# One decoder trunk on one core: maxima's rows handed on one step later, outputs' low halves subtracted by VectorE

## Chip, core and metric

The kernel runs on one core of one Trainium2 chip. The metric is the device time of one execution in microseconds (us), and the time of a kernel is the median of its runs. Engines are named as the profile names them: PE (TensorE matmuls), PEld (its weight loads), DVE (VectorE), ACT (ScalarE), POOL (GpSimd), SP (SyncE, which only issues DMAs here). A profile is one execution, recorded.

## What is computed

A two-layer trunk over 2048 tokens of width 1024: a Mamba-2 mixer, then an attention mixer with 16 heads, 64 + 32 channels for queries and keys and 64 for values, and a final RMS norm. The change touches the causal attention alone, which the reference writes in blocks of 128 queries:

```python
    for i in range(S // Q_BLOCK):
        q0 = i * Q_BLOCK
        kv_len = q0 + Q_BLOCK
        s = jnp.einsum('bqhd,bkhd->bhqk', q_nope[:, q0:kv_len], k_nope[:, :kv_len]) + \
            jnp.einsum('bqhr,bkr->bhqk', q_rope[:, q0:kv_len], k_rope[:, :kv_len])
        s = s.astype(jnp.float32) * scale
        mask = (q0 + local)[:, None] >= jnp.arange(kv_len)[None, :]
        p = jax.nn.softmax(jnp.where(mask, s, -jnp.inf), axis=-1).astype(v.dtype)
        outs.append(jnp.einsum('bhqk,bkhd->bqhd', p, v[:, :kv_len]))
```

The output of a head is later multiplied by a gate and by the output weights. Float32 accuracy is kept by halves: a float32 value is stored as a high float16 part and a low one, its rest, and a product is three matmuls (high by high, high by low, low by high).

## The kernel before

The attention stage is the function `heads`. A job is a head h and a block qb of 512 queries, so a head has four jobs; a step of the main loop handles two key blocks of 128 of one job, so the jobs have 2, 4, 6 and 8 steps and a head has 20. There are 320 steps. The engines' instructions stand in the order in which this function issues them. One step does, mixed with each other:

- **scores** of this step's two key blocks: PE computes transposed scores into bank `s` (lines 1388 to 1390, the causal mask by line 1392), ACT takes the exponential into `x` (1394) and casts it to the high half of `PTs` (1399). The low half is `x` minus the high half, `lows` (1412): POOL does it, 512 columns an instruction; for the steps on the diagonal DVE does it, one step later (896 columns, then 384).
- **values**, two steps behind the scores: PE multiplies `PTs` with the head's values into `o` (1427 to 1429).
- **maxima** of later jobs, eight steps ahead of their scores: PE computes plain scores of 128 queries by up to 512 keys into one of the six `s` banks (1266), DVE reduces them to running minima of the negated scores in `mx` (1268). A bank is free again when DVE is through.
- at the end of the step, `waiting()`, what earlier steps put off to this one.

What is put off, before the change. When the last maximum of job n is made in step k: in step k+1 `part_peaks` splits the four numbers into halves in a small tile `nm` (ACT 1275, then POOL 1276); in step k+2 `rows` turns this tile on DVE (1280, `rT<-nm`) and SP writes it to DRAM (1281, `m_d<-rT`); in step k+3 SP reads it back as two rows of the query tile (1289, `xT<-m_d`), from where the score matmuls add it.

When the last values of a job are done in step k, `finish` computes the reciprocal of the sum and the output `On` on DVE (1443, 1447). In step k+2 ACT casts it to the high half of `Op` (1451) and POOL subtracts to get the low half (1452). For the second head of a pair, in step k+4, `turn` has SP transpose `Op` by a DMA into `Os` (1461). Two steps later POOL adds the two halves to `Of` (1464), and three steps after the turning SP stores it (1470, `o_d<-Of`); the stores of head 13 also load a piece of the output weights (1240, `wr<-in_mla_w_out`), which the last stage, `back`, splits into `W` and `K` halves on ACT (1546) and DVE (1547) while the last heads still run. When the last values of head h are done, SP loads the keys and values of head h+2 into the same buffer (1217, 1218, 1223).

Every engine and SP's queue work in order, so a wait holds up what stands behind it.

Of the kernel before, what the change touches and what calls it, by code (L numbers as in the profile page):

```python
# [13 lines left out]
F16 = mybir.dt.float16  # L14
I32 = mybir.dt.int32
AF = mybir.ActivationFunctionType
ALU = mybir.AluOpType
# [4 lines left out]
P = 128  # L22
# [47 lines left out]
class Net:  # L70
# [1253 lines left out]
    def heads(self, sp):  # L1324
        nc, v, act, mm = self.nc, self.nc.vector, self.nc.scalar.activation, self.nc.tensor.matmul
# [12 lines left out]
        for n, (h, qb) in enumerate(jobs):  # L1338
            for j in range(4):
                parts = self.cuts(qb, j)  # L1340
# [7 lines left out]
        for i in range(len(duos) - 2, -1, -1):  # L1348
            n, kb = duos[i + 1]
# [5 lines left out]
        def bank():  # L1355
            return self.t(self.ap, "s", [P, TB], bufs=6)

        def maxima(n, j, i, c0, w, last):

            h, qb = jobs[n]  # L1360
            if (j, i) == (0, 0):
                peak[n] = self.t(sp, "mx", [P, 4, 4], bufs=4)
                if n + 2 < len(jobs):
                    self.load_q(*jobs[n + 2])
            Q, K, qs = quer[h, qb], keys[h % 2], slice(j * P, (j + 1) * P)
            junk = self.t(sp, "junk", [P, TB], BF16, bufs=1)
            self.peaks(bank(), Q[:, 0, qs], K[:, 0, c0:c0 + w], fence, junk, peak[n], i, j, last)
            if last and j == 3:
                u, e, Q = turned[n % 3], peak.pop(n)[:, i], quer[h, qb]
                given[n] = [(step[0] + 1, lambda: self.part_peaks(e, u)),  # L1370
                            (step[0] + 2, lambda: self.rows(n, u, self.t(sp, "rT", [P, 32], F16, bufs=2), None)),
                            (step[0] + 3, lambda: self.set_rows(n, Q))]

        def scores(n, kb):

# [38 lines left out]
        def values(n, kb, u):  # L1414

            h, qb = jobs[n]
            V = vals[h % 2]
            if kb == 0:
                outs[n] = self.t(self.ap, "o", [P, 4, P], bufs=2)
            for b in range(2):  # L1420
                k = kb + b
                jj = max(k - 4 * qb, 0)
                for j in range(jj, 4):
                    o = outs[n][:, j]
                    at = TB + (j - jj) * P if b else j * P
                    hi, lo = u[:, 0, at:at + P], u[:, 1, at:at + P]
                    mm(o[:, 0:64], hi, V[:, k, 0:64], start=k == 0 and j == 0, stop=False, skip_group_check=True)  # L1427
                    mm(o[:, 0:65], hi, V[:, k, 64:129], start=False, stop=False, skip_group_check=True)  # L1428
                    mm(o[:, 0:65], lo, V[:, k, 64:129], start=False, stop=k == 4 * qb + j, skip_group_check=True)  # L1429
                if b == 0:  # L1430
                    yield
            if kb == 4 * qb + 2:
                finish(n)
            if kb == 4 * NB - 2 and h + 2 < NH:
                self.load_k(h + 2, 0, NB)
                self.load_v(h + 2)

        def finish(n):

            h, qb = jobs[n]  # L1440
            O = outs.pop(n)
            ri = self.t(sp, "ri", [P, 4], bufs=2)
            v.reciprocal(ri, O[:, :, 64])
            if (h // 2, qb) not in pairs:
                pairs[h // 2, qb] = self.t(sp, "Op", [P, 2, 4, P], F16, bufs=6)
            o = self.t(sp, "On", [P, 4, 64], bufs=3)
            v.tensor_tensor(o, O[:, :, 0:64], ri.unsqueeze(2).to_broadcast([P, 4, 64]), ALU.mult)
            hi, lo = (pairs[h // 2, qb][:, m, :, h % 2 * 64:(h % 2 + 1) * 64] for m in range(2))

            def parts():  # L1450
                act(hi, o, AF.Copy)
                nc.gpsimd.tensor_tensor(lo, o, hi, ALU.subtract)

            later.append((step[0] + 2, parts))
            if h % 2:
                later.append((step[0] + TURN + 1, lambda: turn(h, qb)))

        def turn(h, qb):

            o = self.t(sp, "Os", [P, 2, TB], F16, bufs=2)  # L1460
            nc.sync.dma_start_transpose(o.rearrange("p m (j t) -> p (m j) t", j=4),
                                        pairs.pop((h // 2, qb)).rearrange("p m j c -> p (m j c)"))
            whole = self.t(sp, "Of", [P, TB], bufs=2)
            later.append((step[0] + 2, lambda: nc.gpsimd.tensor_tensor(whole, o[:, 0], o[:, 1], ALU.add)))
            later.append((step[0] + 3, lambda: store(h, qb, whole)))

        def store(h, qb, o):

            r0 = (h // 2) * P
            nc.sync.dma_start(self.o_d[r0:r0 + P, qb * TB:(qb + 1) * TB], o)  # L1470
            if h == NH - 3:
                self.load_wo(qb)

        step, later, held, fresh, made, given = [0], [], [], [], ends[2], {}
# [18 lines left out]
        def some(due):  # L1493

            nonlocal made
            while cols[made] < due:
                maxima(*chunks[made])
                made += 1
# [229 lines left out]
```

## Time and profile before

| | |
|---|---|
| median of 3 runs | 2894.04 us (2892.67 to 2894.78) |
| profiled execution | 2886.88 us, of which the span from first to last instruction is 2885.1 us |
| mean granted TensorE clock | 0.994 of full speed |
| busy in the span | PE 97%, PEld 56%, DVE 74%, ACT 63%, POOL 33% |
| the attention stage | from about 1975 us to about 2695 us of the span |

Times in rows of the trace are microseconds from the start of the span. Matmuls overlap: one of 512 columns is recorded with 0.38 us though the next may start 0.22 us after it, so a wait of PE shows as idle time only from the end of the last matmul.

### The profile page before, as it was taken

The page shows a single profiled execution, that of the slowest core. Times are in us where ns is not written, and L with a number is a line of the kernel's source. Part 1 is how long each engine was busy: PE and PEld are TensorE (multiplying, and loading weights), DVE is VectorE, ACT ScalarE, POOL GpSimd, SP SyncE. Part 2 cuts the span into 40 slices and gives each one's busy share as a digit, 9 for nine tenths or more (in the row PEclk, how much of TensorE's full clock was granted, in tenths as well). Part 3 has the DMA queues.
Part 4 walks back from the last instruction along what each step waited for, and adds up shares of the span by engine and source line. Part 5 has one row for each costly group of instructions (what it writes and reads, how often), then busy time and mean ns, then how long its engine had stood idle before and what let it go on. Part 6 is the DMA issues. An engine that isn't in the chain of part 4 may idle for free. (4 is left out here: it accounts for less than half of the span.)

```text
span 2885.1 us, 58276 instructions
## 1 busy us (share of the span) xinstructions
PE 2793.3 (97%) x21170; PEld 1623.6 (56%) x21170; DVE 2124.8 (74%) x5114; ACT 1830.9 (63%) x3989; POOL 961.3 (33%) x1080
## 2 busy tenths in 40 slices
PE   7899999999999999999999999999999999998998
PEld 3465556554555554454555545545666666665787
DVE  7789987787777878879775455357788878878454
ACT  8777655576566766556554344335889888898422
POOL 0221221211121211223221121224778777786300
PEclk9999999999999999999999999999999999999999
DMA  8765736455464567636646988872333324333553
GB/s 292 252 201 197 219 118 208 142 179 183 162 226 132 176 192 223 214 116 209 219 138 231 264 264 247 258 225 68 81 67 73 78 65 88 78 77 99 171 210 110
DMA packets 361156, 487.01 MB, mean 169 GB/s; under 512 B 179490, under 2 KB 224322, under 8 KB 359428
## 3 DMA queue, kind: packets, MB, share of 16 engines
q1 hardware_dynamic: 349732, 447.37, 51.7%
q0 software_dynamic: 11136, 35.92, 3.4%
q8 instruction: 166, 2.72, 0.4%
q14 instruction: 122, 1.00, 0.1%
HBM read 332.83 MB, written 123.34 MB: 158 GB/s over the span
## 5 line engine op out<-in xcount | busy, mean ns | idle before, releaser
L1412 POOL TENSOR_TENSOR PTs<-x,PTs 128x512 f16<-128x512 f32 (+1 forms) x380 | 444.4, 1194 | 135.8 <-ACT PTs L1399 91.3
L1394 ACT ACTIVATE x<-s 128x512 f32<-128x512 f32 (+3 forms) x640 | 326.5, 523 | 70.5 <-PE s L1390 42.8
L86 PE MATMUL mm<-xT,wsp 128*128 128x512 f16 x800 | 305.5, 382 | 5.5 <-ACT wsp L117 5.2
L87 PE MATMUL mm<-xT,wsp 128*128 128x512 f16 x800 | 304.8, 381 | 0.0
L88 PE MATMUL mm<-xT,wsp 128*128 128x512 f16 x800 | 304.0, 380 | 0.0
L1399 ACT ACTIVATE PTs<-x 128x1024 f16<-128x1024 f32 (+1 forms) x320 | 297.2, 929 | 9.9
L1268 DVE CUSTOM_DVE_ANT_0 junk<-s,fence,mx 128x512 bf16<-128x512 f32 (+1 forms) x372 | 241.0, 648 | 47.8 <-PE s L1266 16.9
L1429 PE MATMUL o<-K,PTs 128*128 128x65 f16 x2176 | 263.3, 193 | 4.1 <-DVE PTs L1412 1.7
L1427 PE MATMUL o<-K,PTs 128*128 128x64 f16 x2176 | 265.9, 192 | 0.0
L1428 PE MATMUL o<-K,PTs 128*128 128x65 f16 x2176 | 265.6, 194 | 0.0
L839 POOL TENSOR_TENSOR Xp<-Xw,Xp 128x512 fp32r<-128x512 f32 x64 | 90.6, 1416 | 505.9 <-ACT Xp L838 279.9
L86 PE MATMUL mm<-wsp,xT 128*128 128x512 f16 (+1 forms) x640 | 230.6, 362 | 3.5 <-ACT craw L643 3.4
L87 PE MATMUL mm<-wsp,xT 128*128 128x512 f16 (+1 forms) x640 | 231.2, 361 | 2.1 <-DVE wsp L118 2.1
L1428 PEld LDWEIGHTS <-PTs 128*128 128x128 f16 x2176 | 203.1, 97 | 53.0 <-issue 0.5
L1427 PEld LDWEIGHTS <-PTs 128*128 128x128 f16 x2176 | 205.0, 97 | 49.4 <-issue 2.0
L649 DVE SCALAR_TENSOR_TENSOR cacc<-craw,pack,cacc 128x512 f32<-128x512 f32 x288 | 215.8, 779 | 22.9 <-ACT cacc L647 21.6
L88 PE MATMUL mm<-wsp,xT 128*128 128x512 f16 (+1 forms) x640 | 231.1, 361 | 0.0
L1388 PE MATMUL s<-xT,K 98*128 98x512 f16 (+1 forms) x628 | 219.3, 349 | 10.8 <-DVE mx L1268 6.2
L1389 PE MATMUL s<-xT,K 96*128 96x512 f16 (+1 forms) x628 | 219.5, 350 | 0.0
L1266 PE MATMUL s<-K,xT 96*128 96x512 f16 (+1 forms) x616 | 213.6, 349 | 5.2 <-ACT nm L1275 2.0
L1390 PE MATMUL s<-xT,K 96*128 96x512 f16 (+1 forms) x628 | 217.9, 347 | 0.0
L1429 PEld LDWEIGHTS <-PTs 128*128 128x128 f16 x2176 | 201.7, 98 | 6.7 <-DVE PTs L1412 3.8
(480 smaller groups left out, 7272.1 us busy)
## 6 DMA issues: line engine op xcount, KB each, us to landing
wsp<-wi_d SPq DMA_DIRECT2D x96, 512.0 KB
big<-cumT SPq DMA_DIRECT2D x64, 512.0 KB
wraw<-in_ssm_w_out_dram SPq DMA_DIRECT2D x96, 256.0 KB
wi_d<-wsp SPq DMA_DIRECT2D x32, 512.0 KB
wsp<-wo_d SPq DMA_DIRECT2D x32, 512.0 KB
wsp<-wu_d SPq DMA_DIRECT2D x28, 512.0 KB
hx<-in_ssm_w_in_dram SPq DMA_DIRECT2D x48, 256.0 KB
wraw<-in_ssm_w_in_dram SPq DMA_DIRECT2D x48, 256.0 KB
```

The costliest lines, as they stand in the source:

```text
L86: mm(out, l_hi, r_hi, start=start, stop=False)
L87: mm(out, l_hi, r_lo, start=False, stop=False)
L88: mm(out, l_lo, r_hi, start=False, stop=stop)
L1268: self.nc.vector.tensor_tensor_reduce(junk[:, :w], s[:, :w], fence[:, at:at + w], -1.0 / MSCALE, peak[:, i - 1, j:j + 1] if i else 3.0e38, ...
L1388: mm(s, K[0:98, 0, ks], Q[0:98, 0, c], start=True, stop=False)
L1389: mm(s, K[0:96, 0, ks], Q[0:96, 1, c], start=False, stop=False)
L1394: act(o, s, AF.Exp)
L1399: act(u[:, 0, at:end], x[:, at:end], AF.Copy)
L1412: engine.tensor_tensor(u[:, 1, a:b], x[:, a:b], u[:, 0, a:b], ALU.subtract)
L1427: mm(o[:, 0:64], hi, V[:, k, 0:64], start=k == 0 and j == 0, stop=False, skip_group_check=True)
L1428: mm(o[:, 0:65], hi, V[:, k, 64:129], start=False, stop=False, skip_group_check=True)
L1429: mm(o[:, 0:65], lo, V[:, k, 64:129], start=False, stop=k == 4 * qb + j, skip_group_check=True)
```

## The change

The transposition of the maxima moves from two to three steps behind and the reading of the rows from three to four. The low half of the outputs is made by DVE, one step after ACT's high half. The two turned halves are added three steps after the turning, and stored four after. There is one more buffer for `On`.

```diff
-                            (step[0] + 2, lambda: self.rows(n, u, self.t(sp, "rT", [P, 32], F16, bufs=2), None)),
-                            (step[0] + 3, lambda: self.set_rows(n, Q))]
+                            (step[0] + 3, lambda: self.rows(n, u, self.t(sp, "rT", [P, 32], F16, bufs=2), None)),
+                            (step[0] + 4, lambda: self.set_rows(n, Q))]
...
-            o = self.t(sp, "On", [P, 4, 64], bufs=3)
+            o = self.t(sp, "On", [P, 4, 64], bufs=4)
...
-            def parts():
-                act(hi, o, AF.Copy)
-                nc.gpsimd.tensor_tensor(lo, o, hi, ALU.subtract)
-
-            later.append((step[0] + 2, parts))
+            later.append((step[0] + 2, lambda: act(hi, o, AF.Copy)))
+            later.append((step[0] + 3, lambda: v.tensor_tensor(lo, o, hi, ALU.subtract)))
...
-            later.append((step[0] + 2, lambda: nc.gpsimd.tensor_tensor(whole, o[:, 0], o[:, 1], ALU.add)))
-            later.append((step[0] + 3, lambda: store(h, qb, whole)))
+            later.append((step[0] + 3, lambda: nc.gpsimd.tensor_tensor(whole, o[:, 0], o[:, 1], ALU.add)))
+            later.append((step[0] + 4, lambda: store(h, qb, whole)))
```

Lines behind line 1450 stand three lower in the changed kernel (1464 becomes 1461), and 1451 and 1452 become 1450 and 1451. PE's order is the same in both programs.

The place where one pair of heads passes to the next comes once in two heads. On DVE, before:

```order
L1268 ISA junk_27417,mx_27345<-s_27418,fence_21736,mx_27345 128x128
...
L1268 ISA junk_27429,mx_27345<-s_27430,fence_21736 128x512
...
L1268 ISA junk_27452,mx_27345<-s_27453,fence_21736,mx_27345 128x512
...
L1280 STREAM_TRANSPOSE rT_27468<-nm_4122_21732 128x32
L1268 ISA junk_27482,mx_27345<-s_27483,fence_21736,mx_27345 128x512
...
L1412 TENSOR_TENSOR PTs_27422<-x_27421,PTs_27422 128x896
L1268 ISA junk_27528,mx_27345<-s_27529,fence_21736,mx_27345 128x256
```

The same place on DVE after the change:

```order
L1451 TENSOR_TENSOR Op_26295<-On_27260,Op_26295 128x4x64
L1268 ISA junk_27417,mx_27344<-s_27418,fence_21736,mx_27344 128x128
...
L1268 ISA junk_27429,mx_27344<-s_27430,fence_21736 128x512
...
L1268 ISA junk_27452,mx_27344<-s_27453,fence_21736,mx_27344 128x512
...
L1268 ISA junk_27479,mx_27344<-s_27480,fence_21736,mx_27344 128x512
...
L1412 TENSOR_TENSOR PTs_27422<-x_27421,PTs_27422 128x896
L1280 STREAM_TRANSPOSE rT_27515<-nm_4122_21732 128x32
```

The transposition moved behind one reduction and one subtraction of 896 columns, and a low half of the outputs came in three reductions ahead of it.

SP's queue at the same passing, before:

```order
L1281 DMA m_d<-rT_27468 128x32
L1461 DMA_TRANSPOSE Os_27471<-Op_26297 128x8x128
L1289 DMA xT_26815<-m_d 1x16x32 x2
L1470 DMA o_d<-Of_27473 128x512
L1217 DMA K_3902_20566<-kn_d 64x4096
L1218 DMA K_3902_20566<-kr_d 32x4096
L1223 DMA K_3902_20566<-v_d 128x16x128
L1233 DMA xT_27786<-qn_d 64x2x512
```

And after, on SP:

```order
L1458 DMA_TRANSPOSE Os_27468<-Op_26295 128x8x128
L1281 DMA m_d<-rT_27515 128x32
L1289 DMA xT_26815<-m_d 1x16x32 x2
L1217 DMA K_3902_20566<-kn_d 64x4096
L1218 DMA K_3902_20566<-kr_d 32x4096
L1223 DMA K_3902_20566<-v_d 128x16x128
L1467 DMA o_d<-Of_27470 128x512
L1233 DMA xT_27786<-qn_d 64x2x512
```

The turning went ahead of the maxima's write, and the store of the sum went from ahead of the key and value loads to behind them.

The third place is on ACT where the last pair of heads begins, and the first piece of the last stage's weights (`W<-wr`) stands among the exponentials. Before:

```order
L1394 ACTIVATE x_35353<-s_35355 128x512
L1394 ACTIVATE x_35353<-s_35370 128x512
L1546 ACTIVATE W_37186<-wr_35351 128x2x512
L1399 ACTIVATE PTs_35354<-x_35353 128x1024
L1394 ACTIVATE x_35397<-s_35399 128x512
```

On ACT after the change, rows that begin with the same exponentials and go on until that piece:

```order
L1394 ACTIVATE x_35350<-s_35352 128x512
L1394 ACTIVATE x_35350<-s_35367 128x512
L1399 ACTIVATE PTs_35351<-x_35350 128x1024
...
L1399 ACTIVATE PTs_35582<-x_35581 128x1024
L1394 ACTIVATE x_35634<-s_35636 128x512
L1543 ACTIVATE W_37186<-wr_35391 128x2x512
L1394 ACTIVATE x_35634<-s_35655 128x512
```

The piece moved from row 2692 of ACT to row 2712, into the step six steps later. On DVE its low half moved likewise, from ahead of the other seven such instructions of this stretch to among them: before, those seven stand within 26 rows of DVE, after it all eight stand within 51.

## The prediction

> **What bounds the kernel now.** I read the busy time by stretch first, then who waits for whom in the steady part, then the timeline where those waits are longest. By stretch (length, busy time of PE, PEld, DVE, ACT, POOL with counts, granted clock, DMA share, GB/s):
>
> ```profile
> 2000.00:2600.00 600.00, 591.88 (x7969) 387.03 (x7968) 477.52 (x1358) 530.68 (x925) 467.54 (x463) 1.00 0.35 74
> 2605.00:2610.00 5.00, 1.97 (x22) 1.11 (x21) 2.30 (x8) 1.68 (x2) 0.00 (x0) 0.87 1.00 245
> 2610.00:2615.00 5.00, 4.14 (x41) 3.16 (x41) 4.08 (x10) 4.91 (x10) 4.54 (x5) 0.50 0.88 139
> 2630.00:2635.00 5.00, 3.83 (x46) 2.23 (x45) 4.79 (x8) 3.43 (x7) 2.23 (x3) 1.00 0.86 297
> 2635.00:2640.00 5.00, 3.24 (x20) 1.62 (x20) 5.00 (x10) 4.30 (x6) 4.50 (x4) 0.94 0.47 133
> 2640.00:2645.00 5.00, 5.00 (x50) 2.72 (x48) 4.97 (x12) 4.70 (x8) 4.08 (x4) 0.72 0.60 195
> 2660.00:2695.00 35.00, 32.41 (x504) 22.26 (x503) 20.99 (x34) 33.44 (x58) 33.02 (x27) 1.00 0.19 40
> ```
>
> PE is the bound: 591.88 of 600 us. So the change can win only the time in which PE stands, and removing waits of DVE or POOL is worth nothing unless PE waits for them. Who waits, 2000 to 2600 (total us, times, longest):
>
> ```profile
> DVE rT L1280 <- POOL nm L1276: 47.6, 28, 2.3
> DVE junk L1268 <- PE s L1266: 28.8, 80, 0.5
> POOL Of L1464 <- PE s L1266: 15.6, 4, 3.9
> POOL Of L1464 <- DMA Os<-Op: 8.2, 2, 4.2
> PEld L1389 <- issue: 5.7, 19, 1.0
> PEld L1266 <- issue: 5.2, 5, 1.6
> PEld L1429 <- DVE PTs L1412: 2.4, 9, 0.5
> PE s L1388 <- DVE mx L1268: 2.7, 9, 0.9
> PE s L1266 <- DMA K<-kr_d: 0.5, 1, 0.5
> ```
>
> PE's idle time is 600 - 591.88 = 8.1 us; its weight loader, whose records do not overlap, stands 5.7 + 5.2 + 2.4 = 13.3 us. The truth lies between, nearer to 13.3, because the tail of a matmul's record covers some of each stall. Of it 8.1 (5.7 + 2.4) is DVE being late: a bank not yet reduced, a low half not yet made. 5.2, in five stalls, is PE waiting for the next head's keys. So why is DVE late? The passing from one pair of heads to the next shows it:
>
> ```profile
> 2240.75 0.09 DVE L1268 DVE_READ_ACCUMULATOR2_ANT mx<- 128x1 f32 x1
> 2242.90 0.19 POOL L1276 TENSOR_TENSOR nm<-mx,nm 128x4 f16<-128x4 f32 x1
> 2243.12 0.21 DVE L1280 STREAM_TRANSPOSE rT<-nm 128x32 f16<-128x32 f16 x1 [2.29 <-POOL nm L1276]
> 2243.36 0.33 SPq L1281 DMA_DIRECT2D m_d<-rT  x1
> 2243.78 1.99 SPq L1461 DMA_TRANSPOSE Os<-Op  x1
> 2243.92 1.09 DVE L1412 TENSOR_TENSOR PTs<-x,PTs 128x896 f16<-128x896 f32 x1
> 2246.17 0.55 DVE L1412 TENSOR_TENSOR PTs<-x,PTs 128x384 f16<-128x384 f32 x1
> 2247.27 1.15 POOL L1464 TENSOR_TENSOR Of<-Os 128x512 f32<-128x512 f16 x1 [4.18 <-DMA Os<-Op]
> 2247.31 2.06 DVE L1412 TENSOR_TENSOR PTs<-x,PTs 128x896 f16<-128x896 f32 x1
> 2248.44 0.34 SPq L1470 DMA_DIRECT2D o_d<-Of  x1
> 2248.88 0.52 SPq L1217 DMA_DIRECT2D K<-kn_d  x1
> 2337.04 0.52 SPq L1217 DMA_DIRECT2D K<-kn_d  x1
> 2344.54 0.22 PE L1266 MATMUL s<-K,xT 96*128 96x128 f16 x1 [0.87 <-ACT nm L1275]
> ```
>
> DVE stands 2.29 us for a POOL result that queues behind POOL's subtractions. SP then turns late, POOL waits 4.18 for the turned tile, its addition meets DVE's subtraction (2.06 instead of 1.09), and the store that follows holds the key loads. Two heads later the keys issued at 2337.04 are wanted 7.5 us on, and PE stands 0.87. (A step is (2337.04 - 2248.88) / 40 = 2.2 us.)
>
> **The change, part by part.** *Transposition one step later.* The longest wait, 2.3 us, is about one step, and POOL also loses the outputs' low half. So I cost the 47.6 us at nothing from here on. DVE then reaches its diagonal subtractions up to 2 us earlier; next late would be ACT's cast that feeds them.
>
> *Low half on DVE.* No row shows it. By the clean rows 896 columns take 1.09 and 384 take 0.55, so 1.05 ns a column: 256 columns take 0.55 - 128 x 1.05 ns = 0.42 us. What it can wait for POOL shows in the groups of the steady part:
>
> ```profile
> L1412 DVE TENSOR_TENSOR PTs<-x,PTs 128x896 f16<-128x896 f32 x54 | 71.5, 1323 | 0.0
> L1412 DVE TENSOR_TENSOR PTs<-x,PTs 128x384 f16<-128x384 f32 x53 | 35.6, 672 | 0.0
> L1452 POOL TENSOR_TENSOR Op<-On,Op 128x256 f16<-128x256 f32 x54 | 46.3, 858 | 2.5 <-ACT Op L1451 2.4
> L1412 POOL TENSOR_TENSOR PTs<-x,PTs 128x512 f16<-128x512 f32 x328 | 377.3, 1175 | 100.9 <-ACT PTs L1399 77.0 <-issue 11.8 <-POOL nm L1276 9.9
> ```
>
> DVE's subtractions average 0.23 and 0.12 us above clean, and the worst above (2.06) lost 0.97. So 54 low halves cost DVE from 54 x 0.42 = 23 to 54 x (0.42 + 0.97) = 75 us; I take 0.3 us of waiting, since POOL is busy 78% (467.54 of 600): 39 us, less than the 47.6 it gets back. POOL loses 46.3. The cover is DVE's idle time; if it were gone, each low half would hold the bank of the reduction behind it.
>
> The Trainium skill, page "SBUF — State Buffer", section "Who interferes with whom", states that a VectorE instruction with two SBUF inputs and a GpSimd instruction that reads SBUF exclude each other, the second one fully blocked until the first ends. The 2.06 row, begun 0.04 us after POOL's addition, agrees. The rule speaks against this part: by it each low half that meets POOL waits out POOL's instruction, and the 75 us end would be the one to take; that is the first rival below.
>
> *Addition and store one step later, turning ahead of `m_d`.* The turned tile has landed when POOL comes to it, so the 4.18 us hole and the collision behind it go. The key loads no longer stand behind the store: in their place counts `m_d`, a reading back of the rows, then the keys, and I expect them some 2 us earlier in the odd heads. In the even heads, where no store stood ahead, `m_d` comes under 1 us later. Of the 8.1 us I take 6, of the 5.2 I take 2.5: **-8.5** in the steady part, bounds 0 and -13.3.
>
> *The last stage's first weights on ACT.* These are the rows of the largest stall:
>
> ```profile
> 2602.35 0.60 ACT L1394 ACTIVATE x<-s 128x512 f32<-128x512 f32 x1 [0.46 <-PE s L1390]
> 2603.15 0.41 SPq L1240 DMA_DIRECT2D wr<-in_mla_w_out_dram  x1
> 2608.32 1.06 ACT L1546 ACTIVATE W<-wr 128x1024 fp32r<-128x1024 f32 x1 [5.38 <-DMA wr<-in_mla_w_out_dram]
> 2610.86 0.48 PE L1388 MATMUL s<-xT,K 98*128 98x384 f16 x1 [3.50 <-ACT x L1394]
> ```
>
> ACT stands 5.38 us for a weight load, PE 3.50 behind it, and then the granted clock is 0.50 for five microseconds. The load needs 5.2 us (2603.15 to 2608.32). After the change it is issued behind the key loads, a step or so later, but ACT asks six steps (13 us) later, so it has landed. PE's loss here is (5 - 1.97) + (5 - 4.14) idle and half of 4.14 to the clock: 6.0. I take **-5.5**, bounds -6.0 and 0.
>
> *The other weights, 2630 to 2645.* PE loses 1.17 + 1.76 idle and 0.28 x 5 = 1.4 to the clock, 4.3 in all, with DVE busy 4.8 to 5.0 of 5. The eight extra instructions on DVE stand twice as wide now, but one more is among them, with the low halves, and weights whose store is a step later may hold ACT again: **-1**, bounds -4.3 and +3.
>
> *The end of attention.* PE idles 35 - 32.41 = 2.6 from 2660 to 2695, partly for POOL's subtractions; POOL loses its low halves, DVE gains them with 14 us free: **-0.5**, bounds -2.6 and +1.5. The last chain:
>
> ```profile
> 2696.54 2.84 DVE L1547 TENSOR_TENSOR K<-wr,K 128x1024 fp32r<-128x1024 f32 x2 [0.45 <-ACT K L1546]
> 2696.89 1.40 POOL L1452 TENSOR_TENSOR Op<-On,Op 128x256 f16<-128x256 f32 x1 [0.62 <-ACT Op L1451]
> 2698.32 1.23 SPq L1461 DMA_TRANSPOSE Os<-Op  x1
> ```
>
> The low half now stands on DVE between the two weight halves: the first ends at about 2697.7, plus 0.42 gives 2698.1 instead of 2698.3: **-0.3**, bounds -0.5 and +1.
>
> The buffer more for `On` costs nothing. Sum: -8.5 - 5.5 - 1 - 0.5 - 0.3 = -15.8. The profiled execution took 2886.88 us (span 2885.1), 7.2 below the median of the runs, so the sum gives 2871.1 for such an execution; the same difference on the median of 2894.04 is **2878.2**.
>
> **Rivals.** *Slower: POOL blocks the low halves.* DVE's waits now are 47.6 + 28.8 = 76.4 us, 1.41 for each of the 54 low halves; from there on DVE has nothing left, and 0.42 + 0.97 = 1.39 is close to it. Two of a head's four stand where DVE reduces bank after bank; if 27 of them hold PE for 1 us each, and the steady gain is nil, the time is 2894 + 27 - 7.3 = 2914. For it: POOL's 78%. Against: the present subtractions lose 0.12 and 0.23 on average, not 0.97.
>
> *The keys take over.* With DVE's waits gone PE wants the keys sooner, and in every head they now follow a later `m_d` and its reading back. If the odd heads keep their 2.5 and the seven even ones stand 0.9 each: -15.8 + 2.5 + 6.3 = -7.0, or 2887. For it: 5.2 us of such stalls now. Against: only five waits in some 14 heads (600 us by 20 steps of 2.2), and the store no longer delays the loads.
>
> *The weight stall only moves.* The load issued later and behind the keys keeps ACT standing, there or at the next piece: -15.8 + 5.5 + 1.5 = -8.8, or 2885. Against: 13 us of later asking beside a load of 5.2.
>
> **How the numbers follow.** Forecast 0.68, keys 0.14, weights 0.10, slower 0.08. The modest ends of the terms (-2, -4, +2, +0.5, 0) give 2890.5, the good ends (-12, -6, -3, -1.5, -0.5) give 2871; both middle rivals lie inside, and only the slow one outside: 2870 to 2890. About 0.2%, 5.8 us, is what a measurement of this kernel can tell from no change, so faster means below 2888.2: nearly all of the forecast and over half of the two middle rivals, 0.81; same 0.12; slower 0.07.
>
> **What would show it.** The wait of `rT` for `nm` falls from 47.6 to under 5 us; the low half on DVE averages below 0.8 us; POOL's wait for `Os` is gone; the weight loader's three waits sum to under 6; ACT's 5.38 us wait and the 0.50 clock near 2610 are gone. I am wrong if the low halves average 1.2 us or more, if PE's stalls ahead of line 1266 grow in even heads, or if a wait for `wr` of several microseconds stands on ACT at another place.

## The result and the profile after

The changed kernel takes 2876.62 us (median of 6 runs, 2872.23 to 2877.95) against 2894.84 us (6 runs, 2892.67 to 2900.98): ratio 0.9931, 95% interval 0.9919 to 0.9944. That is 18.2 us less; forecast were 15.8 less. The profiled execution of the changed kernel took 2876.48 us, its span 2874.7.

The saving is split by three marks that both traces have: the first exponential of the stage, the first one of head 13, and the last one. The two rows of each kernel are the group of all 640 exponentials (shortest, median and longest duration in ns, first and last start) and the timeline at head 13. Before:

```profile
L1394 ACT ACTIVATE x<-s x640: 265/578/602, 1976.7 to 2693.2; 128x512 f32<-128x512 f32 x160
2554.34 0.60 ACT L1394 ACTIVATE x<-s 128x512 f32<-128x512 f32 x1 [0.30 <-PE s L1392]
```

After:

```profile
L1394 ACT ACTIVATE x<-s x640: 267/579/603, 1982.0 to 2680.5; 128x512 f32<-128x512 f32 x160
2547.39 0.60 ACT L1394 ACTIVATE x<-s 128x512 f32<-128x512 f32 x1 [0.30 <-PE s L1392]
```

| stretch (us) | before | after | difference | forecast |
|---|---|---|---|---|
| heads 0 to 12 (first exponential to head 13) | 577.6 | 565.4 | -12.2 | -8.5 |
| heads 13 to 15 (to the last exponential) | 138.9 | 133.1 | -5.8 | -7.0 |
| last exponential to the end of the span | 191.9 | 194.2 | +2.3 | -0.3 |
| sum | | | -15.7 | -15.8 |

What lies ahead of the first exponential took 5.3 us longer in the profile after. The change touches nothing there, and over the kernels below this mark lies anywhere from 1976.7 to 1984.1 us. The profile before was 8 us below its median, the one after at its median, so these two executions differ by less than the medians. Each stretch here and below is read from one execution. Kernels that were profiled twice agree to 1.1 us in every stretch; the kernel before has only this one, short execution. One of the five executions of the kernel called "the same again" below took 4814.63 us; without it its median is 2874.56 instead of 2875.05 us.

The busy time of the steady part and of three stretches near the end, after (columns as in the prediction), and the waits of 2000 to 2600 us:

```profile
2000.00:2600.00 600.00, 599.06 (x8109) 392.97 (x8106) 522.44 (x1449) 541.55 (x945) 436.09 (x418) 1.00 0.36 76
2600.00:2615.00 15.00, 15.00 (x218) 10.03 (x216) 13.80 (x41) 14.78 (x29) 11.21 (x12) 1.00 0.75 157
2615.00:2645.00 30.00, 26.00 (x318) 16.27 (x315) 26.89 (x61) 23.52 (x40) 19.27 (x16) 0.94 0.36 116
```

```profile
DVE junk L1268 <- PE s L1266: 26.2, 72, 0.5
PEld L1266 <- issue: 1.9, 3, 1.1
DVE rT L1280 <- POOL nm L1276: 1.4, 1, 1.4
PE s L1266 <- DMA K<-kr_d: 0.6, 1, 0.6
POOL Of L1461 <- DMA Os<-Op: 0.4, 1, 0.4
```

PE stands 0.9 us of 600 where it stood 8.1. DVE no longer waits for `nm` (47.6 before), and the weight loader's rows for lines 1389 and 1429, which spoke of a late DVE (5.7 and 2.4), are gone. The passing of a pair of heads that the prediction showed, now on SP, POOL and DVE:

```profile
2241.32 1.29 SPq L1458 DMA_TRANSPOSE Os<-Op  x1
2245.51 1.15 POOL L1461 TENSOR_TENSOR Of<-Os 128x512 f32<-128x512 f16 x1
2245.59 0.21 DVE L1280 STREAM_TRANSPOSE rT<-nm 128x32 f16<-128x32 f16 x1
2245.82 0.35 SPq L1281 DMA_DIRECT2D m_d<-rT  x1
2250.20 0.52 SPq L1217 DMA_DIRECT2D K<-kn_d  x1
2251.91 4.11 SPq L1467 DMA_DIRECT2D o_d<-Of  x1
```

The turning is issued ahead of `m_d` and the keys ahead of the store. The store now stands 4.11 us on SP, though the addition had ended at 2246.66. In the kernel before, the next load stood as long in the same place, behind the loads of keys and values:

```profile
2250.56 4.17 SPq L1233 DMA_DIRECT2D xT<-qn_d  x1
```

In either kernel, whatever follows these loads stands 2.4 to 5.7 us on SP, all 14 times; the rows do not show what it waits for. The loads behind it appear in no wait of PE between 2000 and 2600.

DVE's groups, 2000 to 2600:

```profile
L1451 DVE TENSOR_TENSOR Op<-On,Op 128x256 f16<-128x256 f32 x55 | 46.0, 836 | 0.0
L1412 DVE TENSOR_TENSOR PTs<-x,PTs 128x896 f16<-128x896 f32 x55 | 66.4, 1207 | 3.0 <-ACT PTs L1399 2.8
L1412 DVE TENSOR_TENSOR PTs<-x,PTs 128x384 f16<-128x384 f32 x56 | 35.9, 641 | 0.0
```

A low half takes 0.84 us on average, half of it beyond the 0.42 that is its clean time (0.41 in the shortest rows).

### The profile page after: what moved, and what is told of

The parts are those of the page before. It is cut to its first block, busy times and chain, and to the rows that moved or that the text cites. A ratio compares the mean times of both kernels' runs of the same rounds, so it can differ in the third digit from the quotient of the medians.

```text
span 2874.7 us, 58315 instructions
## 1 busy us (share of the span) xinstructions
PE 2788.8 (97%) x21170; PEld 1623.9 (56%) x21170; DVE 2160.0 (75%) x5178; ACT 1831.0 (64%) x3989; POOL 910.4 (32%) x1016
## 4 chain that ended last, share of the span: by engine, by line
PE 63%; DVE 14%; issue 10%; DMA 5%; ACT 5%; POOL 2%; SPq 1%; POOLq 0%; DVEq 0%; ACTq 0%
PE mm L86 10%; PE mm L88 10%; PE mm L87 10%; PE s L1388 4%; PE s L1389 4%; PE s L1266 4%; PE s L1390 4%; DVE cacc L649 3%; PE tr L87 3%; PE tr L86 3%; PE tr L88 3%; DMA big<-cumT 2%; PE o L1428 2%; PE o L1429 2%; PE o L1427 2%
## 5 line engine op out<-in xcount | busy, mean ns | idle before, releaser
L1427 PEld LDWEIGHTS <-PTs 128*128 128x128 f16 x2176 | 204.6, 97 | 50.2 <-issue 2.4
L1428 PEld LDWEIGHTS <-PTs 128*128 128x128 f16 x2176 | 202.6, 97 | 53.0 <-issue 0.3
L1389 PE MATMUL s<-xT,K 96*128 96x512 f16 (+1 forms) x628 | 218.7, 348 | 0.0
L86 PE MATMUL mm<-wsp,yT 128*128 128x512 f16 (+1 forms) x512 | 198.3, 387 | 8.2 <-DVE sz L673 7.6
```

The costliest lines, as they stand in the source:

```text
L86: mm(out, l_hi, r_hi, start=start, stop=False)
L1389: mm(s, K[0:96, 0, ks], Q[0:96, 1, c], start=False, stop=False)
```

## Experiments

All kernels but the first two rows were timed in five rounds beside the kernel before, whose median in these sets was 2892.55 to 2895.19 us. "Steady", "last" and "rest" are the three stretches of the table above, in us, from one profiled execution each.

| kernel | median us | ratio to before, 95% | steady | last | rest |
|---|---|---|---|---|---|
| before | 2894.84 | 1 | 577.6 | 138.9 | 191.9 |
| whole change | 2876.62 | 0.9931 (0.9919 to 0.9944) | 565.4 | 133.1 | 194.2 |
| whole change again | 2875.25 | 0.9936 (0.9922 to 0.9950) | 565.2 | 132.0 | 194.9 |
| transposition alone | 2880.32 | 0.9952 (0.9937 to 0.9968) | 571.4 | 133.9 | 192.5 |
| low half alone | 2892.04 | 0.9993 (0.9984 to 1.0002) | 578.4 | 138.6 | 194.6 |
| addition and store alone | 2883.63 | 0.9962 (0.9947 to 0.9977) | 573.2 | 133.6 | 192.1 |
| whole but low half | 2872.69 | 0.9925 (0.9911 to 0.9940) | 564.5 | 132.9 | 194.2 |
| the same again | 2875.05 | 0.9937 (0.9923 to 0.9952) | 565.4 | 132.0 | 193.7 |
| transposition and store | 2876.10 | 0.9942 (0.9929 to 0.9954) | 568.3 | 132.2 | 193.7 |
| whole, low half twice | 2896.18 | 1.0010 (1.0000 to 1.0020) | 581.2 | 134.5 | 197.1 |
| turning first on SP | 2886.58 | 0.9972 (0.9961 to 0.9983) | 574.0 | 137.7 | 194.7 |
| before, weights by hand | 2892.97 | 0.9992 (0.9980 to 1.0003) | 582.9 | 133.5 | 191.6 |
| whole but low half, weights by hand | 2870.90 | 0.9917 (0.9904 to 0.9931) | 567.3 | 128.1 | 192.3 |
| the same, gate's load first | 2869.92 | 0.9921 (0.9906 to 0.9935) | 567.8 | 128.6 | 193.3 |

### The parts alone

The transposition alone, in the kernel before:

```diff
-                            (step[0] + 2, lambda: self.rows(n, u, self.t(sp, "rT", [P, 32], F16, bufs=2), None)),
-                            (step[0] + 3, lambda: self.set_rows(n, Q))]
+                            (step[0] + 3, lambda: self.rows(n, u, self.t(sp, "rT", [P, 32], F16, bufs=2), None)),
+                            (step[0] + 4, lambda: self.set_rows(n, Q))]
```

> The transposition of the maxima one step later, and the rows two lines behind it, nothing else: POOL keeps the outputs' low half, the addition and the store stay where they were. My theory (VectorE is late because it stands 47.6 us for nm): that wait falls under 5 us, and the PE stalls that a late VectorE makes go, 6 of 8.1 us; the keys still queue behind the store, and ScalarE still stands about 5 us for the first output weights, so 2894 - 6 = 2888 us. Rival, the load of POOL: VectorE's wait goes, but the stalls of PE stay, since POOL's subtractions are as late as before: within 2 us of 2894. Rival, the keys: the rows are now written behind the turning, with no later store to make up for it, and the first scores of a head wait: above 2896.

It gave 0.9952, 14 us: over twice what I expected. Its waits, 2000 to 2585 us, and ScalarE's first weights:

```profile
DVE junk L1268 <- PE s L1266: 71.5, 184, 0.8
PEld L1266 <- issue: 6.8, 7, 1.5
PEld L1389 <- issue: 1.4, 3, 0.8
DVE rT L1280 <- POOL nm L1276: 0.8, 1, 0.8
```

```profile
2596.89 0.42 SPq L1240 DMA_DIRECT2D wr<-in_mla_w_out_dram  x1
2601.69 1.06 ACT L1546 ACTIVATE W<-wr 128x1024 fp32r<-128x1024 f32 x1 [2.60 <-DMA wr<-in_mla_w_out_dram]
```

DVE's wait for `nm` (45.3 us over this stretch before) did not go into work: it became waiting for PE (27.1 before, 71.5 now), which is to say spare time. The stalls of a late DVE fell from 5.7 to 1.4 (L1389), those for the keys did not (6.8). What I had not expected: although the weight load kept its place, ScalarE waits 2.60 us for it instead of 5.38, and the last three heads take 5.0 us less.

The low half alone:

```diff
-            o = self.t(sp, "On", [P, 4, 64], bufs=3)
+            o = self.t(sp, "On", [P, 4, 64], bufs=4)
...
-            def parts():
-                act(hi, o, AF.Copy)
-                nc.gpsimd.tensor_tensor(lo, o, hi, ALU.subtract)
-
-            later.append((step[0] + 2, parts))
+            later.append((step[0] + 2, lambda: act(hi, o, AF.Copy)))
+            later.append((step[0] + 3, lambda: v.tensor_tensor(lo, o, hi, ALU.subtract)))
```

> The outputs' low half on VectorE a step later alone (with the one more buffer for its source); maxima and additions stay where they were. My theory: VectorE gains 54 instructions of 0.42 to 0.72 us, 23 to 39 us, and still stands for nm; POOL reaches nm up to 0.86 us sooner in two of a head's four rounds, so that wait falls to 25 to 40 us. Both sides cancel: 2894 within 3 us. Rival, the exclusion of VectorE and POOL: the low halves take over 1.2 us each and hold PE in two of a head's four rounds: 2905 or more. Rival, the load of POOL is the cause of everything: the wait for nm falls under 10 us and the time to 2886 or below.

No difference that this measurement can tell: both sides cancel, as expected. Over the same stretch DVE's wait for `nm` fell from 45.3 to 26.6 us, and its waiting for PE from 27.1 to 9.0: the added work took up both.

The addition and the store alone:

```diff
-            later.append((step[0] + 2, lambda: nc.gpsimd.tensor_tensor(whole, o[:, 0], o[:, 1], ALU.add)))
-            later.append((step[0] + 3, lambda: store(h, qb, whole)))
+            later.append((step[0] + 3, lambda: nc.gpsimd.tensor_tensor(whole, o[:, 0], o[:, 1], ALU.add)))
+            later.append((step[0] + 4, lambda: store(h, qb, whole)))
```

> The addition of the turned halves and the store one step later alone; maxima and low half stay as they were. My theory: POOL's hole of 4.2 us ahead of the addition goes, the keys are no longer behind the store (2.5 us of PE's stalls), and the first output weights are asked for some six steps after their load, so ScalarE's 5.4 us wait near 2608 goes (5.5 us): 2894 - 8 = 2886 us, with VectorE's wait for nm still at 40 us or more. Rival, the weight stall only moves: ScalarE stands for a weight load at one of the next three pieces, and of the 8 only 3 are left: 2891. Rival, the transposition is what brings all: within 2 us of 2894.

It gave 0.9962, 11 us, with the wait for `nm` untouched. Its waits, 2000 to 2585:

```profile
DVE rT L1280 <- POOL nm L1276: 46.0, 28, 2.3
PEld L1389 <- issue: 6.1, 22, 0.6
```

The weight loader's row for line 1266, the keys (5.2 before), is gone altogether; that of the late DVE (6.1) is as before. So the two parts take two different stalls, and neither needs the other.

### Both without the low half

The whole change, with the low half left to POOL:

```diff
-            later.append((step[0] + 2, lambda: act(hi, o, AF.Copy)))
-            later.append((step[0] + 3, lambda: v.tensor_tensor(lo, o, hi, ALU.subtract)))
+            def parts():
+                act(hi, o, AF.Copy)
+                nc.gpsimd.tensor_tensor(lo, o, hi, ALU.subtract)
+
+            later.append((step[0] + 2, parts))
```

> The whole change but for the outputs' low half, which stays on POOL at its old step. My theory (the low half on VectorE costs 39 us of its free time and gives POOL 46 that PE hardly waits for): the PE stalls of the steady part go as with the whole change, and the time is that of the whole change within 3 us: 2877 + 1 = 2878. Rival, POOL is the one that matters: without the relief the wait for nm stays over 10 us, POOL's subtractions hold PE at the end of attention, and the time is 2883 or more. Rival, the low half on VectorE costs (it takes 0.84 us on average, 0.42 of it waiting): without it the kernel is faster than the whole change by 2 us or more, 2874 or below.

It gave 0.9925 (2872.69 us, as by the rival in which the low half costs), against 0.9931 for the whole change. To tell them apart both ran again, beside each other.

> The whole change once more, beside the kernel without its low half on VectorE on the same chip. Both theories: 0.9931 of before, that is some 20 us less, within 3 us; it is the measure for the other three.

> The whole change but for the low half, which stays on POOL at its old step, once more, now beside the whole change. Theory now (the low half on VectorE costs a little, since the first comparison gave 3.9 us in the medians and 1.0 us between the stretches of attention): 1 to 4 us faster than the whole change. Rival (the two are alike, and the first difference came from what lies ahead of attention): within 1 us. Rival (my forecast: POOL's relief helps the end of attention): 1 us slower or more.

2875.25 and 2875.05 us: alike, as the first rival had it and not as I expected, so nothing shows an effect of the low half. Either way the steady part is 12 to 13 us shorter, where the transposition alone gives 6.2 and the later addition alone 4.4: alone, each leaves the other's stall in place. The wait for `nm` is gone without POOL's relief too:

```profile
DVE junk L1268 <- PE s L1266: 70.7, 179, 0.8
DVE rT L1280 <- POOL nm L1276: 0.8, 1, 0.8
```

Moving the low half to VectorE shows no gain here. It takes 44.8 us of DVE between 2000 and 2585, and DVE's spare time falls from 70.7 to 26.2 us. How near that is to the edge shows when it is done twice:

```diff
-            later.append((step[0] + 3, lambda: v.tensor_tensor(lo, o, hi, ALU.subtract)))
+            for _ in range(2):
+                later.append((step[0] + 3, lambda: v.tensor_tensor(lo, o, hi, ALU.subtract)))
```

> The whole change with the outputs' low half made twice on VectorE, with the same result: 64 more instructions, some 54 us of VectorE at the 0.84 us that one takes now. Theory (VectorE stands 76 of 585 us in the steady part and PE does not wait for it): at most 3 us slower than the whole change. Rival (the low half costs what the first comparison gave, 1 to 4 us, and a second costs as much again or more since the cover is nearly used up): 4 to 15 us slower. Rival (each one that meets POOL holds a bank of the reduction): 20 us slower or more.

20.9 us slower than the whole change on the same chip (2896.18 against 2875.25), so my expectation of at most 3 was wrong. Its rows, 2000 to 2585:

```profile
DVE junk L1268 <- PE s L1266: 2.1, 6, 0.5
PEld L1389 <- issue: 9.3, 25, 1.4
L1452 DVE TENSOR_TENSOR Op<-On,Op 128x256 f16<-128x256 f32 x106 | 78.1, 737 | 1.8
```

I had taken DVE's idle time (76 of 585 us) for its spare time. Spare is only what it waits for PE: 26.2 us. The second set costs 78.1 - 44.8 = 33.3 us more there, 7 more than was left, and the waiting is down to 2.1. The steady part grew by 16.0 us, more than those 7, so not all of the spare time can lie where the low halves need it.

My second rival had named this size, 20 us or more, by another cause: low halves that meet POOL and hold a bank. Beyond 0.42 us each, the 106 low halves took 33.6 us and the 54 of the whole change 22.1. So some 11 of the 33.3 us are waiting for POOL, and 22 are clean work. What either cost PE, this run does not separate.

### Addition or store

> The transposition one step later, rows two lines behind, and of the later addition only the store: the addition stays two steps behind the turning, the store goes to four. The low half stays on POOL. Theory (the keys queue behind the store on SyncE, and the addition itself holds nothing that PE needs): the weight loader's stalls ahead of line 1266 fall from 6.8 to about 2 us as with both later, and the time is that of the kernel with both later within 2 us, 0.9925 of before. Rival (the addition is what matters, because POOL stands for the turned tile with its subtractions queued behind): the stalls behind POOL's subtractions stay, and the time is that of the transposition alone, 0.995 of before.

```diff
-            later.append((step[0] + 3, lambda: store(h, qb, whole)))
+            later.append((step[0] + 4, lambda: store(h, qb, whole)))
```

This edit stands beside that of the transposition. 0.9942 lies between the transposition alone and both later, and its interval overlaps both. The weight loader's wait for line 1266 fell to 3.1 us, four fifths of the way from 6.8 to 2.1; its wait behind POOL's subtractions, 1.3 us, stayed. So the store accounts for most of the keys' part. The steady part (568.3 us) is only half way between 571.4 and 565.4, and how much the addition adds stays open.

### The order on SyncE

Why did the transposition alone bring twice its due, and help ScalarE's weights? In the kernel before, where the turning and `m_d` fall in one step, only their order on SP was exchanged:

```diff
+            run(soon)
             give(0, step[0])
-            for at, f in list(later):
+            run(later)
...
-                later.append((step[0] + TURN + 1, lambda: turn(h, qb)))
+                soon.append((step[0] + TURN + 1, lambda: turn(h, qb)))
```

> The kernel before, with one thing exchanged: where the turning and the writing of the maxima stand in the same step, SyncE issues the turning ahead of m_d. Every other engine keeps its order, the transposition keeps its place, and so its wait for nm. Theory now (of what the late transposition costs, part runs through SyncE: m_d waits for rT, the turning stands behind m_d, then POOL, the store, the weight load and the keys are late in turn): POOL's holes of 4.2 us ahead of the addition go, ScalarE's wait near 2600 falls from 5.4 to about 3 us, as with the transposition alone, where the last three heads took 5 us less; the DVE-caused stalls of the steady part stay (weight loader's L1389 wait about 6 us, rT's wait 40 us or more): 2894 - 5 = 2889, between 2886 and 2891. Rival (all of it is VectorE's own 47.6 us): within 2 us of 2894. Rival (the transposition alone brought its 15 us wholly by the order on SyncE): 2882 or less.

0.9972, 7.4 us by the medians, inside what I expected though near its end. Waits, 2000 to 2585:

```profile
DVE rT L1280 <- POOL nm L1276: 45.9, 27, 2.3
PEld L1389 <- issue: 6.9, 15, 0.8
POOL Of L1464 <- DMA Os<-Op: 5.7, 6, 1.5
PEld L1266 <- issue: 1.7, 2, 1.1
```

DVE waits as long as before, but the longest hole of POOL ahead of the addition is 1.5 instead of 4.2 us and the keys' stalls are 1.7 instead of 5.2. So part of the cost of the late transposition ran through SP: `m_d` waits for `rT`, the turning waits behind `m_d`, then the addition, the store, the weight load and the keys are late in turn. One point missed: ScalarE's wait for its first weights fell only to 4.56 us, not to 3, and the last three heads took 1.2 us less, not 5.0. What else the transposition gives there stays open.

### The weights of the last stage

The four weights that are prepared during attention were loaded and split two heads earlier, in halves, at fixed steps:

```diff
-            if h == NH - 3:
-                self.load_wo(qb)
+            if h == NH - 5:
+                self.load_wo(2 + qb)
+                W = self.made[2 + qb] = self.t(self.wo, "W", [P, 2, 2, TB], F32R, bufs=4)
+                raw = self.wraw[2 + qb]
+                for n in range(2):
+                    later.append((step[0] + 6 + 2 * n, lambda n=n: act(W[:, n, 0], raw[:, n], AF.Copy)))
+                    later.append((step[0] + 7 + 2 * n, lambda n=n: v.tensor_tensor(
+                        W[:, n, 1], raw[:, n], W[:, n, 0].bitcast(F32), ALU.subtract)))
+            if h == NH - 3:
+                self.load_wo((0, 1, 6, 7)[qb])
...
```

First in the kernel before, without any of the change:

> The kernel before with the weights prepared by hand as above, and nothing of the change. By my forecast's terms for the weights (6.0 near 2608 and 4.3 from 2630 to 2645): 2893 - 9 = 2884, with ScalarE's wait for a weight load and the half clock near 2610 gone, and the steady part as before. Rival (PE's stalls there are the late VectorE and the queues, which the load only lets show at that place): 2890 or more.

0.9992: nothing, where my terms gave 9 us. Two stretches, this kernel first, then the kernel before:

```profile
2500.00:2600.00 100.00, 95.08 (x1239) 61.00 (x1238) 82.85 (x225) 87.17 (x153) 75.25 (x75) 1.00 0.46 99
2600.00:2645.00 45.00, 42.12 (x564) 27.33 (x561) 35.97 (x96) 35.91 (x65) 33.37 (x33) 1.00 0.52 132
```

```profile
2500.00:2600.00 100.00, 98.16 (x1338) 64.58 (x1335) 77.17 (x220) 87.88 (x154) 77.83 (x78) 1.00 0.38 82
2600.00:2645.00 45.00, 37.77 (x424) 23.14 (x421) 36.89 (x85) 34.08 (x58) 29.34 (x27) 0.89 0.58 154
```

The stall after 2600 does go (7.2 us idle become 2.9, the clock 0.89 becomes 1.00), but the weights' work costs as much where it now stands: PE idles 4.9 instead of 1.8 us there, and the weight loader's wait for a late DVE (line 1389) grew from 0.7 to 4.8. That fits a DVE that was late already. On top of the transposition and the later addition, where DVE has 70 us to spare, the same edit seems to pay:

> The whole change without the low half on VectorE, and the four weights of the last stage that are prepared during attention loaded and prepared two pairs of heads' ends earlier, in halves, at steps written out by hand (each half on ScalarE 6 or 8 steps after its load is issued, on VectorE a step later); the other four weights are loaded where the first four were. Theory (what is left in the stretch after 2600 is the weights: ScalarE's 4.0 us for the load, double-wide subtractions ahead of the reductions, then the clock): PE's idle time and half clock there, some 6 us, go: 2875 - 5 = 2870 against the kernel without low half, 2869 to 2872. Rival (PE stands there for the loads of gated outputs and the queues of the last heads, whatever the weights do): within 1 us of 2875. Rival (the halves hold a reduction or an exponential each where they now stand): 2877 or more.

> The same, and the gate's load issued ahead of the load that waits for the last store of the outputs. Theory (the chain after attention waits for the gate's load, issued 0.4 us behind the outputs' load, and PE's pause of 2.7 to 3.4 us there brings up to 3 us of half clock): 0.4 to 2 us less than without it. Rival (both loads share the engines' time, the outputs' load then lands as late): within 0.5 us.

2870.9 and 2869.9 us: the fastest of all. The last three heads take 128.1 us (132.9 and 132.0 without the edit), the steady part 2 to 3 us more. The intervals of 0.9917 and 0.9921 still overlap those of the same kernel without the edit (0.9925 and 0.9937) and of the whole change, so a gain of some 4 us is likely, not shown. The gate's load ahead of the other made no difference that shows (1.0 us less by the medians, but the higher ratio):

```diff
-                nc.sync.dma_start(o, self.o_d[rows, ts])
                 nc.sync.dma_start(gt, self.gate_d[rows, ts])
+                nc.sync.dma_start(o, self.o_d[rows, ts])
```

## Why the prediction came out right, point by point

- **What bounds, and the 47.6 us wait.** Right: it fell to 1.4 us. The reason was half right. "POOL also loses the outputs' low half" was not needed: without that relief it is 0.8.
- **Low half on DVE.** I priced it at 0.72 us each, 39 us in all; it measured 0.83 and 44.8, inside the bounds and above the 0.8 that I had set as the mark for being right. That PE would not feel it was right, by a margin that I did not see: 26 us of spare time. The first rival, "from there on DVE has nothing left", is what the doubled low half comes near to.
- **The steady part, -8.5.** It measured -12.2, near the end of its range (-13.3). I kept back 2.1 of the late DVE's 8.1 and 2.7 of the keys' 5.2. Measured, nothing is left of the first and 1.9 of the second. I had also put the earlier turning down to "Addition and store one step later, turning ahead of `m_d`". It belongs to the transposition, which takes `m_d` out of the turning's way; on its own that order is worth 7 us by the medians (5 to 11 by the interval).
- **First weights, -5.5, and the other weights, -1.** At its place the stall went as forecast: the 15 us from 2600 lost 6.4 us before (4.1 idle, and 0.21 of 10.9 to the clock) and nothing after. The two stretches before:

```profile
2600.00:2615.00 15.00, 10.90 (x116) 7.03 (x113) 11.11 (x25) 8.63 (x16) 5.69 (x6) 0.79 0.78 166
2615.00:2645.00 30.00, 26.87 (x310) 16.11 (x309) 25.78 (x61) 25.45 (x42) 23.64 (x22) 0.93 0.48 148
```

  But the next weight took over a part, which I had as the third rival and as a sign of being wrong. Three rows: the next piece before, then the piece that I meant after, then the next piece after:

```profile
2632.32 1.06 ACT L1546 ACTIVATE W<-wr 128x1024 fp32r<-128x1024 f32 x1 [1.54 <-DMA wr<-in_mla_w_out_dram]
2607.40 1.05 ACT L1543 ACTIVATE W<-wr 128x1024 fp32r<-128x1024 f32 x1
2622.14 1.06 ACT L1543 ACTIVATE W<-wr 128x1024 fp32r<-128x1024 f32 x1 [3.80 <-DMA wr<-in_mla_w_out_dram]
```

  From 2615 to 2645 PE lost 5.6 us after (4.0 idle and 0.06 of 26 to the clock) and 5.0 before (3.1 and 0.07 of 26.87), so the second term is +0.6, not -1. Rival and forecast both held in part: a wait stands elsewhere (3.80 us, where it was 1.54), but shorter than the 5.38 that went. Also the cause was only partly the place of the load: the transposition alone halved the first wait.
- **The end of attention, -0.5.** About nothing: over the 35 us that end 1.8 us behind the start of the last exponential, PE idles 2.4 us after (2647.3 to 2682.3) and 2.6 before.
- **The last chain, -0.3.** Outside its bounds (-0.5 to +1) in these two executions: the rest of the span took 2.3 us more. PE's pause ahead of the last products grew from 2.49 to 3.27 us, and three microseconds at a low clock followed. Before and after, then the stretch behind the pause after:

```profile
2708.91 0.50 PE L86 MATMUL mm<-W,oT 128*128 128x512 f32 x1 [2.49 <-ACT oT L109]
2696.96 0.50 PE L86 MATMUL mm<-W,oT 128*128 128x512 f32 x1 [3.27 <-ACT oT L109]
2696.96:2699.96 3.00, 3.00 (x8) 2.37 (x9) 1.43 (x2) 0.51 (x1) 0.00 (x0) 0.57 0.98 330
```

  I had no term for the clock here. That the change causes the drop is not shown: the low half alone and the turning first, with the addition and store at their old step, end as late (194.6 and 194.7 us), and the addition and store alone do not (192.1).

- **The keys take over.** No: 1.9 us of such stalls are left of 5.2.

So in these two executions the sum was met to 0.1 us by luck, by errors that cancel: 3.7 us more gained than forecast in the steady part, 1.2 less in the last heads, 2.6 less at the end. By the medians the gain was 18.2 us, 2.4 more than the sum.

## What to carry to other kernels

Read an engine's spare time from its waits for the bounding engine, not from its idle share: here 76 us of idle were 26 to spare, and a job of 33 us more cost 21, so even that was not all usable. Before crediting a gain to the step that was moved, follow the issuing queue: here one that waited for a late instruction held the transfers behind it, and exchanging two entries brought 0.3%. Freeing an engine may pay a second time: the weights by hand gained nothing while it was late (0.9992) and seem to gain some 4 us once it has time, which these runs do not prove.

## What the runs showed of the hardware

How long PE pauses did not alone decide whether the clock fell. With the low half alone PE paused 2.06 us ahead of the last stage's products and fell to half clock soon after; with the transposition alone it paused 3.12 us and kept the full clock. Each kernel's pause, and three microseconds that begin 1.61 us behind it for the first and at once for the second (the number behind the five engines' busy times is the granted clock):

```profile
2713.39 0.50 PE L86 MATMUL mm<-W,oT 128*128 128x512 f32 x1 [2.06 <-ACT oT L109]
2715.00:2718.00 3.00, 3.00 (x8) 2.35 (x8) 1.53 (x3) 0.63 (x1) 0.00 (x0) 0.50 0.82 280
```

```profile
2699.38 0.50 PE L86 MATMUL mm<-W,oT 128*128 128x512 f32 x1 [3.12 <-ACT oT L109]
2699.38:2702.38 3.00, 3.00 (x13) 2.48 (x14) 1.95 (x3) 0.63 (x1) 0.00 (x0) 1.00 0.86 284
```

The kernels of the table whose rest is below 193 us are those that kept the full clock there; all others were granted 0.50 to 0.74 in the three microseconds right behind their pause. The Trainium skill, page "TensorE: Matmul & The Clock Gate", section "Part 1: The HAM clock gate (the "warmup" mystery)", says that the activity window is free-running, so that the moment of a change depends on where in it the work falls; that fits pauses of 2.06 us with a drop and of 3.12 us without. Its idle window of about 3.4 us does not bound the pause: here the clock fell behind one of 2.06 us.

How long DVE waits for POOL is exact. All 64 low halves of the whole change (shortest, median, longest, in ns):

```profile
L1451 DVE TENSOR_TENSOR Op<-On,Op x64: 409/944/1378, 2002.7 to 2685.9; 128x256 f16<-128x256 f32 x64
```

21 began while POOL stood still and took 0.41 us. 40 began while a subtraction or an addition of POOL had 0.36 to 1.10 us to go, and each took that remainder and 0.28 us more (0.64 to 1.38 us). The other three met a 4-column instruction of POOL or its last 0.06 us, and took 0.41 to 0.45 us. The rule of the Trainium skill that the prediction weighed (SBUF — State Buffer, "Who interferes with whom") holds in each of the 40; that the time did not suffer fits the 26 us that DVE still had to spare.
